# Drawing the activation-half steps of a mixer trunk's FFN together and halving one more w_up chunk

## Chip, cores and metric

The kernel runs on one core of a Trainium2 chip. The metric is the device time of one execution in microseconds (us). The engines are TensorE (PE; its weight loads are shown as PEld), VectorE (DVE), ScalarE (ACT), GpSimd (POOL) and SyncE (SP), which issues the loads.

## The reference, cut to what matters

A block of four mixers makes `merged` from `x` (512 tokens, 1024 channels, float32). What the change touches comes behind them:

```python
x = x + merged @ w_out[l]
hn = rmsnorm(x, ffn_norm_g[l])
gu = hn @ w_up[l]
h = jax.nn.silu(gu[..., :FFN_HIDDEN]) * gu[..., FFN_HIDDEN:]
x = x + h @ w_down[l]
```

`FFN_HIDDEN` is 2816, so `w_up` has 22 chunks of 128 gate and 128 up columns.

## The kernel before, in words

All activations are held transposed, channels on the 128 partitions and the 512 tokens along the free side, in eight tiles. Every product is made of three float32r matmuls: each operand is split into a high and a low part (`hi`, `lo`), and high x high, high x low and low x high are added in PSUM (`mm3`, L274). ACT makes a high part with a copy (a CAST in the profile), DVE makes the low part by subtracting.

Weights come in chunks through two `raw` buffers that SP fills, are split into `hi` and `lo`, and are used once. `open_chunk` (L241) hands out the chunk to be used now and the split steps of the next one, so that ACT and DVE split chunk j+1 while PE works on chunk j. Nothing reorders the program: each engine runs its instructions in the order in which this Python code emits them.

The order around the change is:

- **w_out**, four chunks of two output tiles (L1255 to L1271). For each tile nt: 24 matmuls into `m_o`, DVE adds the residual (`x2`, shown as x<-m_o,xo), ACT scales it (`x2f`), ACT and DVE split it (`x2h`, `x2l`), ACT squares it and DVE adds the square.
- **The first w_up chunks are plain** (`N_PLAIN` = 3, j = 0, 1, 2): 24 matmuls of 512 columns for the gate (`fg`) and 24 for the up part (`fu`). Behind chunk 0 come the sum of squares (`ssq`), the inverse norm and its diagonals (`dg`, DVE). Behind the gate matmuls of chunk 1 they are broadcast (`bc`, four matmuls), ACT copies the rows (`rb2`), and `glu_up` of chunk 0 follows: DVE multiplies by rb (`tg`), ACT takes the Silu, DVE multiplies by the up part (`tu`), ACT copies the high part (`hh`), DVE subtracts (`hl`).
- **The other 19 chunks are halved** (`up_halved`, L1294): a 2 x 2 block scheme of the Strassen-Winograd kind with seven products in place of eight. One product (`prod`) is 12 matmuls of 256 columns. The weight chunk has to be added up first: DVE's `sums` and `sum4` overwrite the chunk in `raw` between the splits, so a halved chunk costs DVE and ACT more steps (`ha`, `la`, `sum`, `ha2`, `la2`, `sum4`, `hb`, `lb`, `hc`, `lc`) than a plain one.
- The products share two PSUM tiles. In order they are B11, B21, T2, T1, T3, B22, T4; B11, T2, T3 and T4 all add into the left half of `s_fa`, and what stands there must be copied out or read before the next is added:

```python
        prod(ac, ch.ahi, ch.alo, 0, "B11", first=True)
        emit(st, "ha")
        A.copy(mu[:, h0], ac)
        late[0]()
        emit(st, "la")
        prod(b1, ch.ahi, ch.alo, 2, "B21", first=True)
...
        prod(ac, ch.hi, ch.lo, 0, "T2")
...
        V.tensor_tensor(pa_[:, h1], ac, cn[:, h0], ALU.add)
...
        prod(ac, ch.ahi, ch.alo, 1, "T4")
```

- **The halves of the activations** that the T products read are made by `halves_gen` (L1235), a generator called `prep`, in eight steps: for each k of 0 to 3 a first step (four DVE operations of 256 columns on `xst` and `xsu`, two ACT casts to `xs`) and a second one (two DVE subtractions of 512 columns, `xs`). Before, one step goes out behind each of w_out's tiles 4 to 7, two within chunk 0, and two within chunk 1.

`late` holds the last two steps of a chunk's gated product, `hh` and `hl`; behind the last plain chunk they are left for `up_halved` to emit.

Of the kernel before, what the change touches and what calls it, by code (L numbers as in the profile page):

```python
# [56 lines left out]
N_WARM = 10  # L57
N_HALVED = 2
BC_AT = 7
N_PLAIN = 3  # L60
N_XW = 4
W0_PIECES = {4: 2, 6: 2}
S5_PAR = 48
# [27 lines left out]
def hybrid_trunk(ctx: ExitStack, tc: tile.TileContext, a: dict, out: bass.AP):  # L91
# [25 lines left out]
    def slot(nm):  # L117
        return sp.tile([P, T], F32, tag="s", name=nm_(nm))
# [5 lines left out]
    def main_ps(nm):  # L124
        return pm.tile([P, T], F32, tag="mm", name=nm_("m_" + nm))
# [7 lines left out]
    def split(src, nm, mk=None):  # L133
        mk = mk or slot
        hi = mk(nm + "h")
        lo = mk(nm + "l")
        A.copy(r_(hi), src)
        V.tensor_tensor(r_(lo), src, hi, ALU.subtract)
        return r_(hi), r_(lo)
# [13 lines left out]
    for part in range(2):  # L153
        specs += [
            ("w_up", j, 2048) if j < N_PLAIN else ("w_ups", j - N_PLAIN, 2048)
            for j in range(NH // 2 * part, NH // 2 * (part + 1))
# [84 lines left out]
    def open_chunk():  # L241
        c = used[0]
        used[0] += 1
        while len(loaded) < min(len(ready) + N_RAW, len(specs)):
            load_next()
        steps = {}
        if len(ready) < min(c + 2, len(specs)):
            steps = split_steps()
        return ready[c], steps
# [12 lines left out]
    def next_chunk():  # L262
        c = used[0]
        used[0] += 1
        while len(loaded) < min(len(ready) + N_RAW, len(specs)):
            load_next()
        while len(ready) < min(c + 2, len(specs)):
            if specs[len(ready)][0] == "w_ups":
                flush(split_steps())
            else:  # L270
                split_next()
        return ready[c]

    def mm3(ps, ch, c, nw, acts, k0=0):  # L274
        n = len(acts)
        for k, (ah, al) in enumerate(acts):
            wh, wl = ch.h(k0 + k, c, P, nw), ch.l(k0 + k, c, P, nw)
            PE.matmul(ps, wh, ah, start=k == 0, stop=False)
            PE.matmul(ps, wh, al, start=False, stop=False)
            PE.matmul(ps, wl, ah, start=False, stop=k == n - 1)  # L280
# [84 lines left out]
    def g2(kt):  # L365
        return cols[:, 8 + kt : 9 + kt]
# [5 lines left out]
    def sumsq_add(acc, src):  # L372
        sq = slot("sq")
        A.activation(sq, src, AF.Square)
        if acc is None:
            return sq
        V.tensor_tensor(acc, acc, sq, ALU.add)
        return acc
# [837 lines left out]
    def keep(nm):  # L1216
        n = nm_(nm)
        return fp.tile([P, T], F32, tag=n, name=n)
# [16 lines left out]
    def halves_gen():  # L1235
        for k in range(4):
            a_, b_ = x2f[k], x2f[k + 4]
            for n, kt, hf in (("B11", k, h0), ("B21", k + 4, h0), ("B22", k + 4, h1)):
                xs[n][k] = tuple(x[:, hf] for x in x2g[kt])
            ta, tb = slot("xst"), slot("xsu")  # L1240
            V.tensor_tensor(ta[:, h0], a_[:, h0], a_[:, h1], ALU.subtract)
            V.tensor_tensor(ta[:, h1], b_[:, h1], a_[:, h1], ALU.subtract)
            ha, hb, la, lb = (slot("xs") for _ in range(4))
            A.copy(r_(ha), ta)
            V.scalar_tensor_tensor(tb[:, h0], ta[:, h0], -1.0, b_[:, h1], ALU.mult, ALU.subtract)
            V.scalar_tensor_tensor(tb[:, h1], tb[:, h0], -1.0, b_[:, h0], ALU.mult, ALU.subtract)
            A.copy(r_(hb), tb)
            yield
            V.tensor_tensor(r_(la), ta, ha, ALU.subtract)
            V.tensor_tensor(r_(lb), tb, hb, ALU.subtract)  # L1250
            for n, h, l, hf in (("T1", ha, la, h0), ("T3", ha, la, h1), ("T2", hb, lb, h0), ("T4", hb, lb, h1)):
                xs[n][k] = (r_(h)[:, hf], r_(l)[:, hf])
            yield

    prep = halves_gen()  # L1255
    for c in range(4):
        ch = next_chunk()
        for n in range(2):
            nt = 2 * c + n
            ps = main_ps("o")  # L1260
            mm3(ps, ch, n * P, 256, mg)
            t = keep("x2")
            V.tensor_tensor(t, ps, xo[nt], ALU.add)
            x2.append(t)
            xf = slot("x2f")
            A.activation(xf, t, AF.Copy, scale=g2(nt))
            x2f.append(xf)
            x2g.append(split(xf, "x2"))
            acc = sumsq_add(acc, t)
            if nt > 3:  # L1270
                next(prep)  # L1271
    rb2 = keep("rb2")

# [20 lines left out]
    def up_halved(late):  # L1294
        ch, st = open_chunk()
        pa_, pb_ = side_ps("fa"), main_ps("fb")
        ac, b1, b2 = pa_[:, h0], pb_[:, h0], pb_[:, h1]
        mu, cn = slot("mu"), slot("cn")
# [6 lines that stand above are left out]
        emit(st, "sum")  # L1305
        late[1]()
        emit(st, "ha2", "la2", "sum4")
        prod(ac, ch.hi, ch.lo, 0, "T2")
        A.copy(mu[:, h1], ac)
        prod(b2, ch.hi, ch.lo, 1, "T1", first=True)  # L1310
        emit(st, "hb")
        A.copy(cn[:, h0], b2)
        emit(st, "lb")
        prod(ac, ch.hi, ch.lo, 3, "T3")
        V.tensor_tensor(pa_[:, h1], ac, cn[:, h0], ALU.add)
        emit(st, "hc")
        prod(b2, ch.hi, ch.lo, 2, "B22")
        V.tensor_tensor(mu, mu, pb_, ALU.add)
        V.tensor_tensor(mu, mu, rb2, ALU.mult)
        A.activation(mu, mu, AF.Silu)  # L1320
        flush(st)
        prod(ac, ch.ahi, ch.alo, 1, "T4")
        tu, hi, lo = slot("tu"), slot("hh"), slot("hl")
        hid.append((r_(hi), r_(lo)))

        def high():
            V.scalar_tensor_tensor(tu, pa_, -1.0, mu, ALU.mult, ALU.mult)
            A.copy(r_(hi), tu)

        def low():  # L1330
            V.tensor_tensor(r_(lo), tu, hi, ALU.subtract)

        return high, low

    hk = NH // 2
    for part in range(2):
        hid = []
        late = (lambda: None,) * 2
        for j in range(hk * part, hk * (part + 1)):
            if j >= N_PLAIN:  # L1340
                late = up_halved(late)
                continue
            ch, st = open_chunk()
            emit(st, "ha", "la")
            if "sum" not in st:
                flush(st)
            psg = main_ps("fg")
            mm3(psg, ch, 0, 256, x2g)
            if j == 1:
                bcast_rows(dgs, rb2)  # L1350
                high, low = glu_up(*first)
                high()
                next(prep)
                low()
            elif j == 0:
                next(prep)
            emit(st, "sum", "ha2", "la2", "sum4", "hb", "lb", "hc")
            psu = side_ps("fu") if j < 2 else main_ps("fu")
            mm3(psu, ch, P, 256, x2g)
            if j == 0:  # L1360
                dgs = diags(inv_rms(ssq_mm(acc)[:, 0:4], 4), "r2")
                acc = None
                first = psg, psu
                next(prep)
                continue
            flush(st)
            late = glu_up(psg, psu)
            if j < N_PLAIN - 1:
                late[0]()
                next(prep)  # L1370
                late[1]()
        for nt in range(8 - N_HALVED * part):
            if nt == 0:
                ch, st = open_chunk()
                emit(st, "ha")
                late[0]()
                late[1]()
                flush(st)
            else:
                ch = next_chunk()  # L1380
            ps = main_ps("d")
            mm3(ps, ch, 0, P, hid)
            t = slot("dn")
            V.tensor_tensor(t, ps, rb2, ALU.mult)
            V.tensor_tensor(x2[nt], t, x2[nt], ALU.add)
            if part:
                acc = sumsq_add(acc, x2[nt])
# [78 lines left out]
    nt, ch = last[-1]  # L1466
# [66 lines left out]
def _layout(inp):  # L1533
# [52 lines left out]
    for b, kts in enumerate((4, 2, 4, 4)):  # L1586
# [8 lines left out]
    up = _chunks(wu, 256)  # L1595
    o["w_up"] = up[:N_PLAIN]
    hv = up[N_PLAIN:].reshape(NH - N_PLAIN, P, 2, 4, 2, P).transpose(0, 1, 4, 2, 3, 5)
    o["w_ups"] = np.ascontiguousarray(
        np.stack([hv[:, :, 0, 0], hv[:, :, 1, 1], hv[:, :, 0, 1], hv[:, :, 1, 0]], axis=2)
    ).reshape(NH - N_PLAIN, P, 2048)  # L1600
    wd = f["w_down"][0]
# [21 lines left out]
```

## Time and profile before

| what | us |
|---|---|
| median of 3 runs | 973.35 (972.72 to 973.45) |
| the profiled execution, its own time | 973.13 |
| its span, first to last instruction | 971.2 |
| busy, PE | 960.8 (99% of the span) |
| busy, PE weight loads | 836.2 (86%) |
| busy, DVE | 681.2 (70%) |
| busy, ACT | 419.5 (43%) |

The span leaves out 1.9 us of the profiled execution's time, which lie around it. Busy time counts an engine's instructions alone; whether a busy second engine costs anything is told only by who waits for whom. Times in the rows below are counted from the span's start. An instruction's end as shown can lie after the next one's start, since the engines overlap the end of one with the start of the next, so the step from start to start is what a queue pays for.

### The profile page before, as it was taken

To read this page: it belongs to the slowest core of one execution; us is meant where nothing else is said; L and a number is where in the kernel's file an instruction comes from. 1 tells how busy PE (TensorE), PEld (TensorE's weight loads), DVE (VectorE), ACT (ScalarE), POOL (GpSimd) and SP (SyncE) were. 2 spreads that over 40 slices of the span, in tenths; PEclk is the share of its full clock that TensorE was granted. 3 is DMA by queue.
4 is the path that set the end of the run, shared out by engine and by line. 5 is a ranking of instruction groups with operands and counts; after the bars stand their busy time and mean duration, and the time that the engine had idled before them with its cause. 6 is when DMAs were issued, how large, how long until landed. Compare 5 with 4: busy or idle time off the path is not lost.

```text
span 971.2 us, 14090 instructions
## 1 busy us (share of the span) xinstructions
PE 960.8 (99%) x5578; PEld 836.2 (86%) x5578; DVE 681.2 (70%) x1264; ACT 419.5 (43%) x720; POOL 6.0 (1%) x22
## 2 busy tenths in 40 slices
PE   9999999999999999999999999999999999999996
PEld 7887888988888888887888888889998899999886
DVE  7676666588777976955645556689974389997455
ACT  7443533343446334226433345555542235554231
POOL 1000000000000000000000000000000000000000
PEclk9999999999999999999999999999999999999998
DMA  8532222230113113262342232222322323232212
GB/s 278 190 106 98 92 88 89 68 121 36 65 55 103 55 44 113 99 199 87 127 159 96 104 130 87 92 83 93 125 90 90 108 99 114 88 131 90 90 60 87
DMA packets 38281, 100.27 MB, mean 103 GB/s; under 512 B 14062, under 2 KB 21787, under 8 KB 32456
## 3 DMA queue, kind: packets, MB, share of 16 engines
q1 hardware_dynamic: 37944, 99.12, 30.7%
q8 instruction: 44, 0.72, 0.3%
q10 hardware_dynamic: 272, 0.26, 0.1%
q14 instruction: 21, 0.17, 0.1%
HBM read 94.94 MB, written 4.42 MB: 102 GB/s over the span
## 4 chain that ended last, share of the span: by engine, by line
PE 94%; DVE 2%; DMA 1%; ACT 1%; issue 1%; SPq 0%; DVEq 0%
PE m_g L81 17%; PE m_d L81 12%; PE s_fa L81 11%; PE m_fb L81 8%; PE m_b L81 7%; PE m_qk L81 7%; PE m_sqk L81 5%; PE m_o L81 4%; PE m_v L81 3%; PE m_u L81 3%; PE m_sv L81 2%; PE m_fg L81 2%; PE s_fu L81 1%; PE m_gb L81 1%; PE m_ga L81 1%; PE s_psy L81 1%
## 5 line engine op out<-in xcount | busy, mean ns | idle before, releaser
L81 DVE TENSOR_TENSOR lo<-raw,hi 128x1024 fp32r<-128x1024 f32 (+4 forms) x190 | 194.9, 1057 | 47.1 <-ACT hi L81 46.5
L81 ACT CAST hi<-raw 128x1024 fp32r<-128x1024 f32 (+4 forms) x190 | 167.3, 917 | 83.1 <-PE m_d L81 30.0
L81 PE MATMUL m_g<-xh,hi 128*128 128x512 f32 x256 | 102.6, 401 | 0.0
L81 PE MATMUL m_g<-xh,lo 128*128 128x512 f32 x256 | 100.0, 391 | 0.3 <-DVE lo L81 0.3
L81 PE MATMUL m_g<-xl,hi 128*128 128x512 f32 x256 | 99.7, 389 | 0.0
L81 PE MATMUL m_d<-hh,hi 128*128 128x512 f32 (+1 forms) x198 | 72.5, 366 | 0.0
L81 PE MATMUL m_d<-hl,hi 128*128 128x512 f32 (+1 forms) x198 | 72.4, 366 | 0.0
L81 PE MATMUL m_d<-hh,lo 128*128 128x512 f32 (+1 forms) x198 | 72.3, 365 | 0.0
L81 ACT ACTIVATE gt<-gt 128x512 f32<-128x512 f32 x32 | 20.2, 632 | 107.2 <-DVE gt L81 107.2
L81 PEld LDWEIGHTS m_g<-xh,lo 128*128 128x128 f32 x256 | 48.0, 188 | 11.2 <-DVE lo L81 1.0
L81 PEld LDWEIGHTS m_g<-xh,hi 128*128 128x128 f32 x256 | 48.1, 188 | 11.0 <-issue 1.0
L81 PEld LDWEIGHTS m_g<-xl,hi 128*128 128x128 f32 x256 | 48.1, 188 | 10.7 <-issue 1.0
L81 PE MATMUL s_fa<-xs,hi 128*128 128x256 f32 x304 | 56.4, 283 | 0.0
L81 DVE TENSOR_TENSOR raw<-raw 128x512 f32<-128x512 f32 (+1 forms) x57 | 49.6, 870 | 2.0
L81 PEld LDWEIGHTS s_fa<-xs,hi 128*128 128x128 f32 x304 | 47.4, 192 | 0.0
L81 DVE TENSOR_TENSOR gt<-m_b,gt 128x512 f32<-128x512 f32 x24 | 16.6, 690 | 38.3 <-PE m_b L81 33.1
L81 DVE TENSOR_TENSOR dn<-m_d,rb 128x512 f32<-128x512 f32 x14 | 9.7, 691 | 47.9 <-PE m_d L81 47.9
L81 PE MATMUL s_fa<-xs,lo 128*128 128x256 f32 x152 | 43.0, 283 | 0.0
L81 PEld LDWEIGHTS m_d<-hh,lo 128*128 128x128 f32 x198 | 37.3, 189 | 6.1
L81 PEld LDWEIGHTS m_d<-hh,hi 128*128 128x128 f32 x198 | 37.3, 189 | 6.0
L81 PEld LDWEIGHTS m_d<-hl,hi 128*128 128x128 f32 x198 | 37.3, 189 | 6.0
L81 ACT ACTIVATE prob<-prob,nmx 128x128 f32<-128x128 f32 (+1 forms) x48 | 20.1, 419 | 49.3 <-DVE nmx L81 49.2
(404 smaller groups left out, 2463.6 us busy)
## 6 DMA issues: line engine op xcount, KB each, us to landing
raw<-in_w_ups SPq DMA_DIRECT2D x19, 1024.0 KB, 4.8
raw<-in_w_g SPq DMA_DIRECT2D x24, 768.0 KB, 4.3
raw<-in_w_in SPq DMA_DIRECT2D x17, 1024.0 KB, 6.6
raw<-in_w_down SPq DMA_DIRECT2D x16, 704.0 KB, 4.1
raw<-in_w_g SPq DMA_DIRECT2D x8, 640.0 KB, 4.5
raw<-in_w_out SPq DMA_DIRECT2D x4, 1024.0 KB, 4.9
raw<-in_w_up SPq DMA_DIRECT2D x3, 1024.0 KB, 4.8
raw<-in_w_glu SPq DMA_DIRECT2D x2, 1024.0 KB, 4.8
```

The costliest lines, as they stand in the source:

```text
L81: return f(out, *args, **kw)
```

## The change

`N_PLAIN` goes from 3 to 2, so chunk 2 is halved and only chunks 0 and 1 are plain; its weights lie in `w_ups` (20 chunks) in place of `w_up` (2). The eight steps of `prep` go out earlier: one behind each of w_out's tiles 4 and 5, two behind each of tiles 6 and 7, and two within chunk 0. None are left within chunk 1. Chunk 1 is now the last plain one, so its `late` steps go to `up_halved`, and chunk 2's halved split falls into the time of chunk 1.

```diff
-N_PLAIN = 3
+N_PLAIN = 2
...
             acc = sumsq_add(acc, t)
-            if nt > 3:
+            for _ in range((nt > 3) + (nt > 5)):
                 next(prep)
...
                 high, low = glu_up(*first)
                 high()
-                next(prep)
                 low()
```

**DVE at the end of w_out.** `x_890` is the residual sum of w_out's last tile, `x2l` its low part; `xs_5436` and `xs_5437` are the second step for k = 1. Before:

```order
L81 SCALAR_TENSOR_TENSOR xsu_5431<-xsu_5431,x2f_5375 128x256
L81 TENSOR_TENSOR x_890_5467<-m_o_5442,xo_4687 128x512
L81 TENSOR_TENSOR x2l_5472<-x2f_5469,x2h_5471 128x512
L81 TENSOR_TENSOR sq_5174<-sq_5174,sq_5475 128x512
L81 TENSOR_TENSOR xs_5436<-xst_5430,xs_5434 128x512
L81 TENSOR_TENSOR xs_5437<-xsu_5431,xs_5435 128x512
```

Now:

```order
L81 SCALAR_TENSOR_TENSOR xsu_5431<-xsu_5431,x2f_5375 128x256
L81 TENSOR_TENSOR xs_5436<-xst_5430,xs_5434 128x512
L81 TENSOR_TENSOR xs_5437<-xsu_5431,xs_5435 128x512
L81 TENSOR_TENSOR x_890_5469<-m_o_5444,xo_4687 128x512
L81 TENSOR_TENSOR x2l_5474<-x2f_5471,x2h_5473 128x512
L81 TENSOR_TENSOR sq_5174<-sq_5174,sq_5477 128x512
```

The two subtractions moved from behind the last tile's sum to ahead of it; behind these rows now follow both steps for k = 2.

**DVE from the first gated product to the next.** Before, `hl_5668` ends the gated product of chunk 1, the rows from `alo_5678` to `lo_5676` split the first halved chunk (chunk 3), and `tg_5740` begins the gated product of chunk 2:

```order
L81 TENSOR_TENSOR hl_5668<-tu_5663,hh_5667 128x512
L81 TENSOR_TENSOR alo_5678<-raw_5577,ahi_5677 128x1024
L81 TENSOR_TENSOR raw_5577<-raw_5577 128x2x512
L81 TENSOR_TENSOR raw_5577<-raw_5577 128x512
L81 TENSOR_TENSOR alo_5678<-raw_5577,ahi_5677 128x512
L81 TENSOR_TENSOR raw_5577<-raw_5577 128x512
L81 TENSOR_TENSOR lo_5676<-raw_5577,hi_5675 128x1024 x2
L81 TENSOR_TENSOR tg_5740<-m_fg_5681,rb_895_5480 128x512
```

Now `tg_5630` to `hl_5636` are the gated product of chunk 0, the rows from `alo_5596` on split the first halved chunk (chunk 2), and `tg_5673` begins the gated product of chunk 1:

```order
L81 TENSOR_TENSOR alo_5596<-raw_5495,ahi_5595 128x1024
L81 TENSOR_TENSOR tg_5630<-m_fg_5503,rb_901_5494 128x512
L81 TENSOR_TENSOR tu_5631<-s_fu_5540,tg_5630 128x512
L81 TENSOR_TENSOR hl_5636<-tu_5631,hh_5635 128x512
L81 TENSOR_TENSOR raw_5495<-raw_5495 128x2x512
L81 TENSOR_TENSOR raw_5495<-raw_5495 128x512
L81 TENSOR_TENSOR alo_5596<-raw_5495,ahi_5595 128x512
L81 TENSOR_TENSOR raw_5495<-raw_5495 128x512
L81 TENSOR_TENSOR lo_5594<-raw_5495,hi_5593 128x1024 x2
L81 TENSOR_TENSOR tg_5673<-m_fg_5599,rb_901_5494 128x512
```

The first halved chunk's sums and low parts now stand between the gated products of chunks 0 and 1, where before they stood between those of chunks 1 and 2.

**ACT at the same place.** `mu_...<-s_fa` is the copy that takes B11 out of `s_fa`. Before, ahead of the first halved chunk's:

```order
L81 CAST hh_5667<-tu_5663 128x512
L81 CAST ahi_5677<-raw_5577 128x1024
L81 CAST ahi_5677<-raw_5577 128x512
L81 CAST hi_5675<-raw_5577 128x1024 x2
L81 ACTIVATE tg_5740<-tg_5740 128x512
L81 CAST ahi_5751<-raw_5673 128x1024
L81 COPY mu_5755<-s_fa_5753 128x256
```

Now:

```order
L81 CAST hh_5635<-tu_5631 128x512
L81 CAST ahi_5595<-raw_5495 128x512
L81 CAST hi_5593<-raw_5495 128x1024 x2
L81 ACTIVATE tg_5673<-tg_5673 128x512
L81 CAST ahi_5684<-raw_5591 128x1024
L81 COPY mu_5688<-s_fa_5686 128x256
```

The copy stands behind a Silu, as before; the Silu is now that of chunk 1, and its input is the row `tg_5673` that closes DVE's list above.

## Rows read from the trace of the kernel before

**Rows 1.** The page, busy time by engine: us, share of the span, instructions

```profile
PE 960.8 (99%) x5578; PEld 836.2 (86%) x5578; DVE 681.2 (70%) x1264; ACT 419.5 (43%) x720; POOL 6.0 (1%) x22
```

**Rows 2.** Chain of waits, w_up's start: start, length, engine and tile

```profile
629.58 0.89 PE s_bc L81 x8
...
655.45 3.01 PE s_fa L81 x24
...
665.66 2.88 PE s_fa L81 x24
...
675.74 2.88 PE s_fa L81 x24
```

**Rows 3.** Waits of PE over the whole span: total, times, longest

```profile
PE s_ssq L81 <- ACT sq L81: 1.4, 1, 1.4
```

**Rows 4.** Timeline of DVE, end of w_out: start, length, idle time ahead

```profile
612.75 0.43 DVE L81 SCALAR_TENSOR_TENSOR xsu<-xsu,x2f 128x256 f32<-128x256 f32 x1
613.09 0.68 DVE L81 TENSOR_TENSOR x<-m_o,xo 128x512 f32<-128x512 f32 x1
615.22 0.69 DVE L81 TENSOR_TENSOR x2l<-x2f,x2h 128x512 fp32r<-128x512 f32 x1 [1.44 <-ACT x2h L81]
...
616.43 0.68 DVE L81 TENSOR_TENSOR xs<-xst,xs 128x512 fp32r<-128x512 f32 x1
617.03 0.69 DVE L81 TENSOR_TENSOR xs<-xsu,xs 128x512 fp32r<-128x512 f32 x1
```

**Rows 5.** Timeline of ACT, end of w_out

```profile
613.21 0.62 ACT L81 CAST xs<-xsu 128x512 fp32r<-128x512 f32 x1 [0.18 <-DVE xsu L81]
```

**Rows 6.** Timeline of PE's weight loads, plain chunks 0 and 2, first halved chunk

```profile
616.91 0.19 PEld L81 LDWEIGHTS m_fg<-x2l,hi 128*128 128x128 f32 x1
...
635.56 0.19 PEld L81 LDWEIGHTS m_fg<-x2h,hi 128*128 128x128 f32 x1
...
646.44 0.19 PEld L81 LDWEIGHTS s_fa<-x2h,ahi 128*128 128x128 f32 x1
...
649.42 0.31 PEld L81 LDWEIGHTS s_fa<-xs,hi 128*128 128x128 f32 x2
...
655.33 0.30 PEld L81 LDWEIGHTS s_fa<-xs,ahi 128*128 128x128 f32 x2
```

**Rows 7.** Timeline of DVE, plain chunks 0 to 2, first halved chunk

```profile
624.01 0.16 DVE L81 TENSOR_SCALAR ms<-s_ssq 128x4 f32<-128x4 f32 x1 [2.55 <-PE s_ssq L81]
...
625.30 0.88 DVE L81 TENSOR_SCALAR dg<-cst,rr 128x128 f32<-128x128 f32 x4
...
631.13 0.69 DVE L81 TENSOR_TENSOR tg<-m_fg,rb 128x512 f32<-128x512 f32 x1 [1.47 <-ACT rb L81]
...
640.79 1.95 DVE L81 TENSOR_TENSOR raw<-raw 128x1024 f32<-128x1024 f32 x2
...
646.34 0.68 DVE L81 TENSOR_TENSOR tg<-m_fg,rb 128x512 f32<-128x512 f32 x1
...
654.85 0.43 DVE L81 TENSOR_TENSOR s_fa<-s_fa,cn 128x256 f32<-128x256 f32 x1
```

**Rows 8.** Timeline of ACT, plain chunks 0 and 1, first halved chunk

```profile
622.12 1.28 ACT L81 ACT_TABLE_LOAD   x1
...
630.50 0.59 ACT L81 COPY rb<-s_bc 128x512 f32<-128x512 f32 x1 [4.15 <-PE s_bc L81]
...
633.79 0.62 ACT L81 CAST hh<-tu 128x512 fp32r<-128x512 f32 x1 [0.76 <-DVE tu L81]
...
648.53 0.36 ACT L81 COPY mu<-s_fa 128x256 f32<-128x256 f32 x1
```

**Rows 9.** Stretches: length, busy us (count) of PE, PEld, DVE, ACT, POOL, PEclk, DMA

```profile
656.90:727.60 70.70, 70.70 (x591) 70.70 (x590) 63.40 (x81) 37.46 (x61) 0.00 (x0) 1.00 0.31 106
```

**Rows 10.** The same view, the span's end

```profile
960.00:965.00 5.00, 2.24 (x18) 1.96 (x17) 3.92 (x14) 0.68 (x2) 0.00 (x0) 1.00 0.55 184
965.00:966.00 1.00, 0.29 (x3) 0.10 (x1) 1.00 (x3) 0.37 (x1) 0.22 (x1) 0.73 0.39 131
```

## The prediction

> **What bounds the kernel now.** I read the page's busy times first: TensorE is busy 99% of the span, VectorE 70% [rows 1]. Then the chain of waits for the stretch around the change: from the plain chunks to the halved ones it is TensorE alone, one product behind the other [rows 2]. The list of TensorE's waits says the same: its longest wait of the whole span is 1.4 us, at the very end [rows 3]. So a microsecond taken off TensorE here is a microsecond gained, and a microsecond for which it has to wait is one lost in full. Whether it has to wait is not told by VectorE's 70%, which is a mean. I therefore read the timelines of DVE, ACT and the weight loads between 611 and 656 us, and asked for each edge how long before its use an operand is ready.
>
> **What is gained.** One plain chunk becomes a halved one. From the first weight load of plain chunk 2 to that of the first halved chunk it is 646.44 - 635.56 = 10.88 us [rows 6]; halved chunks repeat every 675.74 - 665.66 = 10.08 us [rows 2]. Gain: 0.80 us. Nothing else leaves TensorE's queue. The eight steps for the activation halves are only moved, and they belong to other engines. SP's loads keep their order; the one for chunk 3 starts later, because the split of chunk 1 frees its buffer later, but it is not read before chunk 2 runs on TensorE. I cost it at nothing: its cover is most of the time that plain chunk 1 takes, some 10 us.
>
> **First cost: the last tile of w_out.** The two subtractions for k = 1 now stand ahead of the last tile's sum on DVE. The first can start at 613.09, where the sum starts now [rows 4]. The second needs ACT's cast, which ends at 613.21 + 0.62 = 613.83 [rows 5], and starts at about 613.87. One such subtraction occupies DVE for 0.60 us (616.43 to 617.03), so the sum starts at 614.47, which is 1.38 us later than at 613.09, and the low part `x2l`, which hangs on it through ACT, moves from 615.22 to 616.60 and ends at 617.29 [rows 4]. TensorE's load for the first matmul that reads it is at 616.91 [rows 6]. A load follows its releaser by about 0.05 us (the addition into `s_fa` ends at 654.85 + 0.43 = 655.28 [rows 7], the load that waits for it comes at 655.33 [rows 6]), so it comes at 617.34: **0.43 us of waiting**. Bounds: 0, if only the matmul a little behind the load has to wait, and 0.43. I take 0.43, since the row at 655.33 shows the load itself waiting.
>
> **Covered: the norm.** Ahead of the norm DVE now also has the 1.38 us from above, four operations for k = 2 of about 0.34 (612.75 to 613.09 [rows 4]) and two of 0.60, in all 3.94 us. It was idle for 2.55 us there, waiting for the sum of squares [rows 7], so 1.39 are left. And ACT's table load of 1.28 us [rows 8], which lay in that idle time, now queues behind the casts. The diagonals end at 625.30 + 0.88 = 626.18 before [rows 7] and at about 628.9 now; the broadcast on TensorE starts at 629.58 [rows 2]. It is covered by 0.7 us, so I cost it at nothing; if the cover is gone, what is missing is paid in full. Bounds: 0 to 0.5.
>
> **Main cost: the wait of T2 in the first halved chunk.** The product T2 adds into the same columns as B11, so it must wait until ACT has copied B11 out. In ACT's order that copy stands behind the Silu of the last plain chunk, whose input is DVE's `tg`; in DVE's order `tg` stands behind the whole split of the first halved chunk. In the trace of before this just fits: `tg` at 646.34 [rows 7], the copy ends at 648.53 + 0.36 = 648.89 [rows 8], T2's first load at 649.42 [rows 6], 0.53 us to spare. Now the two sides move by unequal amounts.
>
> TensorE's side: the first halved chunk begins at 635.56 in place of 646.44 [rows 6], 10.88 us earlier, and with the 0.43 us from above T2 wants to start at 649.42 - 10.88 + 0.43 = 638.97.
>
> The copy's side: the split can go on only behind `hl` of chunk 0, and `hl` hangs on the broadcast, which TensorE reaches no earlier than before. The broadcast's copy starts at 630.50, and over `tg` (631.13 [rows 7]) and Silu the high part `hh` ends at 633.79 + 0.62 = 634.41 [rows 8]; plus 0.43 this is 634.84. Then `hl` at 634.88, and one slot of 0.60 us later the sums at 635.48. From the sums to the next `tg` the same instructions stand as before: 646.34 - 640.79 = 5.55 us [rows 7], so `tg` starts at 641.03. From `tg` to the end of the copy it takes 648.89 - 646.34 = 2.55 us, so the copy ends at 643.58 and T2 starts at 643.63. **TensorE waits 4.66 us** for it (0.3 of it perhaps already in B21, for the second low part; the sum stays). Bounds from the handovers on this path, some ten of 0.04 us and one Silu: 4.3 to 5.0.
>
> **What is late next.** T4 waits for DVE's addition into `s_fa`, which before ends 8.94 us behind `tg` (655.28 less 646.34 [rows 7]); now 649.97, so T4 comes at 650.02. From T2's load to T4's it takes 655.33 - 649.42 = 5.91 us [rows 6], of which 0.13 is a wait for this same addition (the piece of 24 matmuls takes 3.01 us there and 2.88 later [rows 2]); 643.63 + 5.78 = 649.41. T4 waits 0.61 us, less the 0.13 that the first halved chunk pays already: **0.48 us** more. Bounds: -0.13, if it finds no wait at all, to 0.5. Behind it DVE has a little more time than it needs: in the halved chunks it is busy 63.40 of 70.70 us [rows 9], about 9.0 of 10.08 per chunk, so the lag should be gone one chunk later.
>
> **Sum.** -0.80 + 0.43 + 4.66 + 0.48 = +4.77 us. The profiled execution took 973.13 us, which gives **977.9 us**. It lies 0.2 us below the median of 973.35, a difference too small to matter. The bounds give -0.80 + 0 + 4.3 - 0.13 = +3.4 to -0.80 + 0.43 + 0.5 + 5.0 + 0.5 = +5.6, that is 976.5 to 978.7. For the chances I count 0.2%, 1.95 us, as about what a measurement of this kernel can tell from no change.
>
> **Rival 1, not slower: the wait is not there.** If T2 were not held by the copy, or if DVE were done with the split earlier, the change would bring just its 0.80 us: 972.3, or 972.8 with the wait for `x2l`. The place is ACT's copy of B11, and the point that decides is when the second `tg` starts on DVE: 2.55 us before 638.92, that is by 636.4, nothing is paid. For it: DVE is idle for 1.47 us ahead of the first `tg` [rows 7], so there is room. Against it: that room lies ahead of the broadcast, while the sums stand behind `hl` in DVE's order, at 635.48; 0.9 us would be left for what takes 5.55. Chance 7%.
>
> **Rival 2: the clock falls in the gap.** TensorE would stand still for over 4 us, three times its longest wait so far [rows 3]. In the trace the clock is at its upper level, 2.4 GHz, through all stretches with dense work; at the span's end, with TensorE busy 2.24 us of 5, it still is, and in the microsecond behind that its mean is 0.73, a mix of the two levels [rows 10]. So a stretch of little work does bring it down to 1.2 GHz, and the new gap lies between the two cases that the rows show. If it falls, the first products behind the gap run at half speed. Twelve matmuls take 1.44 us at the upper level (24 in 2.88 [rows 2]), so one or two such products cost 1.44 to 2.88 us, less the 0.48 of T4's wait, which would be hidden: 978.9 to 980.3. Chance 25%.
> The Trainium skill has a rule on this in TensorE: Matmul & The Clock Gate, section "HAM oscillation — how this bites in real kernels": a wait between bursts of matmuls lets the clock gate go back to the half rate, and the next burst starts cold. By that rule, rival 2 would be the outcome; no row of before shows so long a wait amid dense work.
>
> **Rival 3: the lag stays.** DVE keeps only about 1 us of slack per halved chunk [rows 9], and T4 had none in the first. If T4 waited 0.13 to 0.6 us in each of three more chunks, it would add 0.4 to 1.8: 978.3 to 979.7. Against it: each wait of TensorE gives DVE the same time back. Chance 10%.
>
> **How the numbers follow.** My forecast has 58%: 977.9, own range 976.5 to 978.7. The range reaches from 976.5 up to 980.2, over rival 3 and nearly all of rival 2; rival 1 and a remainder stay out. Slower by over 0.2% takes in the forecast, rivals 2 and 3: 0.90, with a little off for errors that I don't see. Rival 1 is within 0.2%: 0.07. Faster by over 0.2% would need more than twice the gain that the chunk can bring: 0.03.
>
> **What would show it.** Right: in TensorE's waits a new one of 4 to 5 us at `s_fa`, released by ACT's `mu`, at about 639 to 644; DVE's second `tg` at about 641; a gap of some 0.4 us at `x2l` near 617; halved chunks of 10.08 us again from the second or third on. Rival 2 would show as a granted clock below 1.00 near 644 and first products of more than 1.44 us. The prediction is wrong if T2's first load comes before 640, or if the span changes by less than 2 us.

## The result and the profile after

The change takes 979.55 us (median of 6 runs, 978.64 to 980.24) against 973.36 us before (6 runs): a ratio of 1.0064, 95% interval 1.0051 to 1.0077. It is slower by 6.2 us, within the range of 976.5 to 980.2 and 1.65 us above the time forecast. The profiled execution is the longest of the six: 980.24 us with a span of 978.3, 7.1 more than before.

The weight loads of TensorE between the plain chunks and the second halved one, in the timeline of the change (start, length, and in brackets the idle time ahead and what ended it):

```profile
617.10 0.19 PEld L81 LDWEIGHTS m_fg<-x2l,hi 128*128 128x128 f32 x1 [0.48 <-DVE x2l L81]
...
635.71 0.19 PEld L81 LDWEIGHTS s_fa<-x2h,ahi 128*128 128x128 f32 x1
...
637.81 0.19 PEld L81 LDWEIGHTS m_fb<-x2h,alo 128*128 128x128 f32 x1 [0.25 <-DVE alo L81]
...
643.34 0.50 PEld L81 LDWEIGHTS s_fa<-xs,hi 128*128 128x128 f32 x2 [4.29 <-ACT mu L81]
...
645.87 0.54 PEld L81 LDWEIGHTS m_fb<-xs,hi 128*128 128x128 f32 x2
...
648.42 0.54 PEld L81 LDWEIGHTS s_fa<-xs,hi 128*128 128x128 f32 x2
...
650.29 0.19 PEld L81 LDWEIGHTS m_fb<-x2h,hi 128*128 128x128 f32 x1
...
651.73 0.31 PEld L81 LDWEIGHTS s_fa<-xs,ahi 128*128 128x128 f32 x2
```

These rows answer to [rows 6]. The first is the wait for the last tile's low part, 0.48 us of idle loading. The first halved chunk begins at 635.71 (B11). T2 should follow its B11 by 649.42 - 646.44 = 2.98 us as in [rows 6], at 638.69; it comes at 643.34, 4.65 us late, of which 0.25 is already spent within B21. Behind it T2 and T1 take 645.87 - 643.34 = 2.53 and 648.42 - 645.87 = 2.55 us in place of 1.44, T3 1.87. B22 takes 1.44 again, and T4 starts without a wait.

On the other side of that wait stand DVE and ACT. The timeline of DVE:

```profile
634.60 0.69 DVE L81 TENSOR_TENSOR hl<-tu,hh 128x512 fp32r<-128x512 f32 x1 [0.69 <-ACT hh L81]
635.21 1.94 DVE L81 TENSOR_TENSOR raw<-raw 128x1024 f32<-128x1024 f32 x2
637.07 0.68 DVE L81 TENSOR_TENSOR alo<-raw,ahi 128x512 fp32r<-128x512 f32 x1
637.79 0.69 DVE L81 TENSOR_TENSOR raw<-raw 128x512 f32<-128x512 f32 x1
638.40 2.43 DVE L81 TENSOR_TENSOR lo<-raw,hi 128x1024 fp32r<-128x1024 f32 x2
640.74 0.68 DVE L81 TENSOR_TENSOR tg<-m_fg,rb 128x512 f32<-128x512 f32 x1
...
650.68 0.43 DVE L81 TENSOR_TENSOR s_fa<-s_fa,cn 128x256 f32<-128x256 f32 x1 [1.35 <-PE s_fa L81]
```

and of ACT:

```profile
641.46 0.63 ACT L81 ACTIVATE tg<-tg 128x512 f32<-128x512 f32 x1 [1.89 <-DVE tg L81]
641.99 1.03 ACT L81 CAST ahi<-raw 128x1024 fp32r<-128x1024 f32 x1
642.93 0.36 ACT L81 COPY mu<-s_fa 128x256 f32<-128x256 f32 x1
```

From `hl` to the second `tg` DVE has no gap. ACT idles 1.89 us for that `tg`, and the copy of B11 ends at 643.29, 0.05 us ahead of T2's first load. The addition into `s_fa`, which was to hold up T4, now itself waits 1.35 us for TensorE.

Why TensorE is slow behind the gap shows in the stretches of the change (length; busy us and count of PE, PEld, DVE, ACT, POOL; granted clock; DMA share, GB/s):

```profile
639.10:643.30 4.20, 0.16 (x2) 0.00 (x0) 3.26 (x5) 2.31 (x5) 0.00 (x0) 0.91 0.33 80
643.30:649.40 6.10, 6.05 (x28) 6.06 (x29) 5.93 (x7) 2.88 (x6) 0.00 (x0) 0.50 0.29 120
649.40:652.00 2.60, 2.60 (x24) 2.60 (x23) 0.43 (x1) 0.79 (x1) 0.00 (x0) 1.00 0.00 0
```

The granted clock is 0.50, the lower of its two levels (1.2 GHz), from before the end of the gap until about 649.4, for 28 matmuls; then it is back at 2.4 GHz.

### The profile page after: what moved, and what is told of

Read it like the earlier page. It is cut to its first block, busy times and chain, and to the rows that moved or that the text cites. A ratio compares the mean times of both kernels' runs of the same rounds, so it can differ in the third digit from the quotient of the medians.

```text
span 978.3 us, 14176 instructions
## 1 busy us (share of the span) xinstructions
PE 963.7 (99%) x5614; PEld 840.1 (86%) x5614; DVE 686.7 (70%) x1271; ACT 421.7 (43%) x725; POOL 6.0 (1%) x22
## 4 chain that ended last, share of the span: by engine, by line
PE 57%; issue 38%; DMA 1%; DVE 1%; ACT 1%; SPq 0%; POOLq 0%; POOL 0%; DVEq 0%
PE m_g L81 17%; PE m_b L81 7%; PE m_qk L81 7%; PE m_sqk L81 4%; PE m_v L81 3%; PE m_o L81 3%; PE m_u L81 3%; PE m_sv L81 2%; PE m_gb L81 1%; PE m_ga L81 1%; PE s_psy L81 1%; PE s_sbo L81 1%; PE s_z L81 1%; DMA raw<-in_w_in 1%; PE s_sc L81 1%
## 5 line engine op out<-in xcount | busy, mean ns | idle before, releaser
L81 PE MATMUL s_fa<-xs,hi 128*128 128x256 f32 x320 | 60.8, 288 | 4.1 <-ACT mu L81 4.1
L81 PEld LDWEIGHTS s_fa<-xs,hi 128*128 128x128 f32 x320 | 51.2, 197 | 4.3 <-ACT mu L81 4.3
L81 DVE TENSOR_TENSOR raw<-raw 128x512 f32<-128x512 f32 (+1 forms) x60 | 52.2, 870 | 2.0
L81 PE MATMUL s_fa<-xs,lo 128*128 128x256 f32 x160 | 45.9, 287 | 0.0
```

The lines of the kernel that those rows point to most:

```text
L81: return f(out, *args, **kw)
```

## The experiments

The theories. **A**: what counts is how much VectorE has to do between the broadcast of the norm and the second `tg`; halving chunk 2 put the split of a halved chunk into that stretch, and the copy of B11 only passes the lag on. **B**: the place of that copy in ScalarE's queue is the cost by itself. **C**: the clock takes a part of its own. A further rival is that drawing the steps together is what costs.

Each edit is shown against the change, and `...` stands for lines left out. Each time is a median, and the ratio compares it with the kernel before, run beside it.

### Drawn together, three chunks plain

```diff
-N_PLAIN = 2
+N_PLAIN = 3
...
                 late[0]()
-                next(prep)
                 late[1]()
```

> The steps stay drawn together into w_out's last four tiles and chunk 0, but three w_up chunks stay plain as before the change. Theory A (VectorE's lag at the first halved chunk is the cost, and it comes from halving chunk 2): the first halved chunk comes 10.9 us later, VectorE has caught up, no wait at the copy of B11; only the wait for x2l of w_out's last tile is left, about 0.4 us: 973.6 to 974.0, clock 0.997. Rival (drawing the steps together is the cost by itself, through the norm's chain or through ACT's queue): 975 or more, with a wait of 1 us or more before the first halved chunk.

973.49 us (10 runs) against 973.30, ratio 1.0003 (0.9993 to 1.0012). Of TensorE's weight loads between 616 and 666 us just one waits:

```profile
617.05 0.19 PEld L81 LDWEIGHTS m_fg<-x2l,hi 128*128 128x128 f32 x1 [0.47 <-DVE x2l L81]
```

There is no wait at `s_fa`, so drawing the steps together does not bring the large one. Its own cost, the row above, is too small for the runs to resolve: the median lies 0.1 us below the stretch that I expected.

### Two chunks plain, steps spread as before

```diff
-            for _ in range((nt > 3) + (nt > 5)):
+            if nt > 3:
                 next(prep)
...
                 high()
+                next(prep)
                 low()
+                next(prep)
```

> Two plain chunks as in the change, but the steps are spread as before: one behind each of w_out's tiles 4 to 7, two within chunk 0, the last two within chunk 1, around hl of its gated product. Theory A: the last two steps add about 2 us of VectorE work between the broadcast and the second tg, so the wait at the copy of B11 grows from 4.3 to about 6.3 us, the wait for x2l goes away (0.4), the clock falls as it does in the change: 980.5 to 982. Rival (drawing together is what costs): the time falls to 977 or below.

981.32 us (4 runs, 979.28 to 982.55), ratio 1.0080 (1.0065 to 1.0095). The wait for `x2l` is gone; the other has grown to 2.14 + 4.28 = 6.42 us, about as theory A has it:

```profile
638.68 0.19 PEld L81 LDWEIGHTS m_fb<-x2h,alo 128*128 128x128 f32 x1 [2.14 <-DVE alo L81]
644.22 0.50 PEld L81 LDWEIGHTS s_fa<-xs,hi 128*128 128x128 f32 x2 [4.28 <-ACT mu L81]
```

In the change the waits at the same loads are 0.25 and 4.29 us, with 0.48 for `x2l`: 5.02 us. So with two plain chunks drawing the steps together helps by the trace: it takes work out of the stretch behind the broadcast. It does not take out enough. The times point the same way, but the two sets of runs overlap (978.64 to 980.24 in the change).

### The gap filled

```diff
+        if part == 0 and len(hid) == N_PLAIN:
+            for _ in range(32):
+                PE.matmul(b2, ch.ahi[:, 0:P], xs["B11"][0][0], start=True, stop=True, skip_group_check=True)
         prod(ac, ch.hi, ch.lo, 0, "T2")
```

> The change, with 32 matmuls of 256 columns put ahead of T2 in the first halved chunk; what they write is overwritten by T1's first matmul. They take 32 x 0.12 = 3.84 us of the 4.3 us in which TensorE stands still. Theory C (the gap lets the clock fall, and the slow products behind it cost about 2.5 us, against 0.5 to 0.6 of a wait of T4 that they hide): granted clock 0.997, T2 still begins 4.2 to 4.5 us late, T4 waits 0.5 to 0.6 us, 977.5 to 978.2. Rival (the clock costs nothing, since VectorE's lag would hold TensorE up by as much anyway): 979.2 to 979.9, with T3, B22 or T4 waiting for what the clock cost before.

978.12 us (4 runs), ratio 1.0047 (1.0030 to 1.0063), 1.4 us under the change. The rows:

```profile
639.36 3.91 PEld L81 LDWEIGHTS m_fb<-x2h,ahi 128*128 128x128 f32 x32
643.73 0.30 PEld L81 LDWEIGHTS s_fa<-xs,hi 128*128 128x128 f32 x2 [0.45 <-ACT mu L81]
...
650.12 0.30 PEld L81 LDWEIGHTS s_fa<-xs,ahi 128*128 128x128 f32 x2 [0.52 <-DVE s_fa L81]
```

T2 starts as late as ever (this trace runs 0.37 us behind that of the change, as the load that waits for `alo` shows: 638.18 against 637.81). But the clock stays up (1.00 in every stretch from 636 to 666 us), and T4 now waits for DVE's addition. Its first load comes 650.12 - 643.73 = 6.39 us behind T2's, 0.61 more than 5.78, which is what the prediction worked out; 0.52 of it shows as idle time. This is the case that the prediction took as the likeliest, and its time is 0.2 us off. It shows that the clock cost the change 1.4 us net; every run here is shorter than every run of the change.

### The copy ahead of the Silu

```diff
+            if j == N_PLAIN - 1:
+                box = []
+
+                def first_late(psg=psg, psu=psu):
+                    box.append(glu_up(psg, psu))
+                    box[0][0]()
+
+                late = first_late, lambda: box[0][1]()
+                continue
             late = glu_up(psg, psu)
```

> The change, with the gated product of plain chunk 1 emitted behind the copy of B11, so that ACT's copy no longer stands behind that Silu; VectorE's order is as in the change. Theory A (VectorE's lag, which the copy only passes on): T2 starts on time but for some 0.4 us (first low part of the split), and the same lag comes back in pieces, about 2 us at T3 (second copy behind hh), 2 us at B22 (copy cn behind the cast that follows VectorE's sums) and 0.6 us at T4; in all 4 to 5 us. If the clock holds over the shorter gaps 977.5 to 978.3, if it falls 979 to 980. Rival B (the copy's place in ACT's queue is the cost): 972.5 to 974.

977.56 us (4 runs), ratio 1.0044 (1.0029 to 1.0059). The waits of 0.25 and 4.29 us have become five:

```profile
638.13 0.19 PEld L81 LDWEIGHTS m_fb<-x2h,alo 128*128 128x128 f32 x1 [0.25 <-DVE alo L81]
641.15 0.30 PEld L81 LDWEIGHTS s_fa<-xs,hi 128*128 128x128 f32 x2 [1.77 <-ACT mu L81]
644.63 0.30 PEld L81 LDWEIGHTS s_fa<-xs,hi 128*128 128x128 f32 x2 [0.55 <-ACT mu L81]
647.71 0.19 PEld L81 LDWEIGHTS m_fb<-x2h,hi 128*128 128x128 f32 x1 [1.59 <-ACT cn L81]
649.71 0.30 PEld L81 LDWEIGHTS s_fa<-xs,ahi 128*128 128x128 f32 x2 [0.51 <-DVE s_fa L81]
```

They sum to 4.67 us. Theory B falls: take the copy out of the Silu's way, and the lag comes back at T2, T3, B22 and T4. The pieces were not as expected. T2 still waited 1.77 us and not 0.4, because the copy stands behind ACT's cast of the next chunk, and that behind a cast which waits for DVE's sums. The clock stays up over these waits (1.00 from 638 to 652 us). That is the larger part of the 2.0 us by which this version is faster than the change: with the gap filled, the clock alone gave 1.4. Where the rest comes from was not followed up.

### The sums in VectorE's idle time

```diff
-                high, low = glu_up(*first)
+                high, low = glu_up(*first, lambda: emit(st, "sum", "ha2"))
                 high()
+                emit(st, "la2", "sum4")
                 low()
```

Within `glu_up` the steps handed over go out between the Silu and `tu`.

> The change, with the first halved chunk's sums and second low part put into the gaps in which VectorE waited for ScalarE within the gated product of chunk 0 (1.25 us ahead of tu, 0.69 ahead of hl), in place of behind hl. Nothing else moves. Theory A (what counts is how much VectorE has to do from the broadcast to the second tg): the second tg starts about 2.1 us earlier, at 638.6, T2 waits about 2.5 us in place of 4.3, B21 no longer waits, T4 still 0.5 to 0.6. If the clock holds over a gap of 2.5 us: 975.7 to 976.4; if it falls: 977.5 to 978.5. Rival (the total of VectorE's work in the stretch counts, not its place): no less than 977 with the clock up.

976.14 us (5 runs), ratio 1.0035 (1.0022 to 1.0048). The second `tg` starts at 638.19 in place of 640.74 (0.35 us of that lies in this trace as a whole, which runs ahead by as much at the load of `x2l`). B21 no longer waits, T2 waits 2.38 us:

```profile
640.79 0.50 PEld L81 LDWEIGHTS s_fa<-xs,hi 128*128 128x128 f32 x2 [2.38 <-ACT mu L81]
```

DVE does the same work as in the change, only earlier, so its place counts and not its total. That bears theory A out and narrows it: the work between the broadcast and the second `tg` is as much as before, and only DVE's idle time in that stretch shrank. What counts is when DVE comes to the second `tg`. Half of the expectation was wrong, though: the time came out as for a clock that holds, while the clock fell:

```profile
638.30:640.80 2.50, 0.32 (x4) 0.12 (x2) 1.56 (x3) 1.90 (x4) 0.00 (x0) 0.98 0.58 144
640.80:644.00 3.20, 3.20 (x15) 3.20 (x16) 3.13 (x4) 1.23 (x3) 0.00 (x0) 0.50 0.51 215
```

The fall was short, some 15 matmuls, and T4's wait was hidden under it, so it cost less than I had put on it: T4's first load comes at 647.98, 7.19 us behind T2's, 1.41 more than 5.78, where T4's wait alone would have been 0.61.

### The norm early, and two versions of it

```diff
+    A.activation(warm, ones[:, 0:1], AF.Sqrt)
...
+            if nt in (5, 7):
+                next(prep)
             x2g.append(split(xf, "x2"))
             acc = sumsq_add(acc, t)
-            for _ in range((nt > 3) + (nt > 5)):
+            if nt in (4, 6):
                 next(prep)
...
+            if j == 0:
+                psg = main_ps("fg")
+                mm3(psg, ch, 0, 256, x2g)
+                ssq = ssq_mm(acc)
+                next(prep)
+                dgs = diags(inv_rms(ssq[:, 0:4], 4), "r2")
+                acc = None
+                A.activation(warm, ones[:, 0:1], AF.Silu)
+                next(prep)
+                flush(st)
+                psu = side_ps("fu")
+                mm3(psu, ch, P, 256, x2g)
+                bcast_rows(dgs, rb2)
+                next(prep)
+                late = glu_up(psg, psu, (lambda: next(prep),))
+                late[0]()
+                continue
             emit(st, "ha", "la")
+            late[1]()
```

The code for the norm and the first gated product within chunk 1 goes away. The edit does three things at once: the norm comes earlier, the activation steps lie elsewhere, and ACT's tables are loaded ahead of their use (the two `warm` lines).

> Two plain chunks as in the change, with the norm ahead: the sum of squares goes out behind the gate matmuls of chunk 0 and the broadcast behind its up matmuls, 6 us earlier than in the change, the activation steps lie one behind each of w_out's tiles 4 to 7 (the second ones in the 1.44 us in which VectorE waits for x2h) and the other four within chunk 0, and ScalarE's tables are loaded ahead of their use. Theory A (VectorE's work between broadcast and second tg is the cost, and TensorE's 10.88 against 10.08 us the gain): no wait of TensorE above 0.3 us from 612 to 660, clock 0.997, 972.2 to 973.0, ratio below 1. Rival (VectorE is too full to split a halved chunk during chunk 1 wherever the broadcast stands): a wait of 1 us or more at s_fa remains, 974 or more.

974.10 us (11 runs), ratio 1.0010 (1.0001 to 1.0019): by its numbers the rival's case. The waits left are 1.09 us at T2 and 0.52 at T4, and DVE's timeline shows a gap that I had put there myself:

```profile
627.79 0.69 DVE L81 TENSOR_TENSOR tu<-s_fu,tg 128x512 f32<-128x512 f32 x1
630.11 1.23 DVE L81 TENSOR_TENSOR alo<-raw,ahi 128x1024 fp32r<-128x1024 f32 x1 [1.64 <-ACT ahi L81]
...
637.40 0.68 DVE L81 TENSOR_TENSOR tg<-m_fg,rb 128x512 f32<-128x512 f32 x1
```

DVE reaches the split 1.64 us before ACT has cast its first half, since in ACT's order `hh` stood ahead of that cast. Turning the two round is the second version:

```diff
-                late[0]()
                 continue
-            emit(st, "ha", "la")
+            emit(st, "ha")
+            late[0]()
+            emit(st, "la")
             late[1]()
```

> As the run before with the early norm, but ScalarE casts the first half of chunk 2's weights (ahi) ahead of hh, where in that run VectorE waited 1.64 us for it. Theory A: the second tg on VectorE comes about 1.6 us earlier (from 637.40 to 635.8), the copy of B11 ends at 638.3, ahead of T2, and the waits of T2 (1.09 us) and T4 (0.52 us) go away: 972.3 to 972.9 with no wait of TensorE above 0.2 us from 612 to 660, ratio 0.9985 to 0.9998. Rival (something else holds T2, so that the wait stays where it is): 973.8 to 974.4, as in that run.

972.48 us (11 runs) against 973.16 for the kernel before beside it, ratio 0.9991 (0.9982 to 1.0000). Not one weight load between 605 and 680 us waits. The chain of waits runs through TensorE alone:

```profile
624.78 5.48 PE m_fg L81 x24
630.26 5.44 PE s_fu L81 x24
635.70 1.43 PE s_fa L81 x12
637.13 1.44 PE m_fb L81 x12
638.57 1.44 PE s_fa L81 x12
...
644.33 3.02 PE s_fa L81 x24
...
654.55 2.88 PE s_fa L81 x24
```

DVE's second `tg` and ACT's copy in that run:

```profile
635.22 0.68 DVE L81 TENSOR_TENSOR tg<-m_fg,rb 128x512 f32<-128x512 f32 x1
```

```profile
637.41 0.36 ACT L81 COPY mu<-s_fa 128x256 f32<-128x256 f32 x1
```

T2's first load:

```profile
638.29 0.31 PEld L81 LDWEIGHTS s_fa<-xs,hi 128*128 128x128 f32 x2
```

The copy ends at 637.77, 0.52 us ahead of that load. From the first matmul of chunk 0 to the first of w_down TensorE takes 726.56 - 612.06 = 114.50 us in the chain of waits, in the kernel before 727.60 - 612.30 = 115.30: the 0.80 us of the halved chunk are all there. The interval of the runs touches 1, so against the kernel before it is the trace that shows the gain; against the change, 7 us, there is no doubt.

## Why the prediction was right, and where it was not

The change is slower, and its time lies in the stated range. It does not lie in the forecast's own range of 976.5 to 978.7: the stated range holds it only because it was drawn over rival 2, which had 25%.

**The gain**: right. In the last version, where nothing waits, it comes out at 0.8 us.

**First cost, `x2l`**: predicted 0.43. The first halved chunk begins at 635.71 in the change; the two traces run 0.24 us apart already where w_out starts (its first load is at 568.16 in the change and 568.40 before), so it is 635.71 - 635.56 + 0.24 = 0.39 us late.

**Norm covered**: right. No load waits for the broadcast.

**Main cost, T2**: predicted 4.66, measured 4.65, of which 0.25 in B21 where the prediction had put 0.3. The path was as drawn: broadcast, `tg`, `hh`, `hl`, split, second `tg`, copy. An agreement within 0.01 us is luck where the bounds were 4.3 to 5.0.

**T4**: predicted 0.48 more. It did not come in the change, since the slow products gave DVE the time; with the gap filled T4 came 0.61 us late, less the 0.13 that was there before, which is the 0.48.

**The clock**: this is the step that failed. The forecast took 58% for a clock that holds over the gap, and 25% for one that falls; it fell. Rival 2 had place and mechanism, and its time of 978.9 to 980.3 holds the measured 979.55. From T2's first load to T4's it took 651.73 - 643.34 = 8.39 us in place of the 5.78 of the prediction: 2.61 us. Its price was built on a product that takes twice as long; at the lower level the product takes 2.53 us against 1.44, so it is 1.1 us per product and not 1.44, and it was nearly two and a half products and not one or two. The two errors offset each other, so that rival 2's time holds the measured one is in part luck. Rival 2 and the Trainium skill's rule agree with the trace here (TensorE: Matmul & The Clock Gate, section "HAM oscillation — how this bites in real kernels": after a long wait between bursts the next burst starts cold): 0.50 from 643.30 to 649.40.

In sum for the profiled execution: -0.80 + 0.39 + 4.65 + 2.61 - 0.13 = 6.72 us. The first matmul of w_down comes at 733.95 in place of 727.43, 6.52 us later, with the 0.24 us from above 6.76. The rest of the span's 7.1 lies in its tail, in the last broadcast of TensorE. Before and in the change:

```profile
964.13 1.16 PE L81 MATMUL s_bc<-cst,rr 128*128 128x128 f32 x8 [1.34 <-DVE rr L81]
```

```profile
970.65 2.08 PE L81 MATMUL s_bc<-cst,rr 128*128 128x128 f32 x8 [1.33 <-DVE rr L81]
```

The second ran at a granted clock of 0.50, the first at 1.00, and from the start of this row to the span's end it is 7.65 against 7.07 us. This 0.58 us is not the change's: the long row also stands in the traces of three plain chunks drawn together, of the filled gap and of the first version with the norm early, the short one in the other four. The six runs' median lies 6.2 us above before and the profiled run 7.1; whether this row is the difference is not shown.

Rival 1 fell with the trace of the change itself, where T2 waits 4.29 us for `mu`, and theory B with the run in which the copy was moved. Rival 3 did not show: T4 waited once at most.

## What to carry to other kernels

Before moving work to a busy engine, follow the one chain that cannot move (here: broadcast, gated product, split, copy) through each engine's own order, and count what stands behind its start; an engine's mean share says nothing of it. A stall of TensorE amid dense work can have two prices, the wait and the products behind it at the lower clock (so here at 4.29 and 2.38 us). Where the wait can't be removed, filling it or breaking it up took the second one away. Where the second engine is the limit, look for a way to start the chain earlier: with the norm six microseconds ahead, the activation steps and table loads placed to suit it and one cast put ahead of `hh`, the loss of 6 us became the gain that the change was after. Of these only the cast's share was measured by itself (974.10 to 972.48 us).

## What was not expected of the hardware

The clock fell in a wait of 2.38 us amid dense work, and in one of 4.29, while it held over waits of 1.77 and 1.59 us some 5 us apart. At the span's end the same work gave both: before, the clock held over 5 us in which TensorE was busy for 2.24 [rows 10], and in the change it had fallen ahead of the last broadcast, behind waits of the same length (1.42 and 1.33 us). So the length of a wait alone does not tell whether the clock falls. At the lower level a product of 12 matmuls takes 2.53 us, 1.76 times and not twice the 1.44. The stretch at the lower level differed in length: 28 matmuls in the change, some 15 behind the shorter gap. The six runs of the change lie 1.6 us apart and the six beside them 0.75, but 16 later runs of the kernel before lie 1.9 apart (972.12 to 974.03), so a wider spread of the change is not shown. The version with the steps spread does spread more: its four runs lie 3.3 us apart, and their mean granted clock falls as their time rises, from 0.994 at 979.28 to 0.990 at 982.55. That fits a stretch at the lower level that differs from run to run; only one of the four was traced, so it is not shown.
